# Two projections side by side on small weight pieces at the start, and five banks, paired stores and four tiles on GpSimd at the end of an encoder layer

## The chip, the cores and the metric

The kernel runs on one core of one Trainium2 chip. The metric is the device time of one execution in microseconds. Three executions of the kernel before took 2081.0, 2082.01 and 2082.91 us; the median is 2082.01 us. TensorE (PE), ScalarE (ACT), VectorE (DVE), GpSimd (POOL) and SyncE (SP, which here only issues DMAs) each work through an instruction queue of their own in order.

## The reference

One encoder layer on 512 tokens with 2048 features, all float32. Cut to what matters here:

```python
xn = rms_norm(x, attn_norm_g)
u_val, u_gate, q, k, v = split(xn @ w_in)          # 1024 + 1024 + 3 * 1024 columns
y_conv = silu(layer_norm(depthwise_conv31(u_val * sigmoid(u_gate))))
y_na = neighborhood_attention(q, k, v, rpb)        # 16 heads of 64, grid 8 x 64, window 8 x 16
x = x + concat(rms_norm(y_conv), rms_norm(y_na)) @ w_out
up = depthwise_conv3(rms_norm(x) @ w_up)           # 2 * 5632 columns
x = x + (silu(gate) * val) @ w_down                # gate, val = halves of up
return rms_norm(x, final_norm_g)
```

## The kernel before, in words

Everything is kept transposed: a tile is 128 features (partitions) by 512 tokens, so x is 16 tiles. Every matrix product is made in three matmuls of a reduced float32 format (`mm3`, L117): each operand is split into a high part (a copy on ACT, rounded to that format) and a low part (a subtraction on DVE), and high by high, high by low and low by high are accumulated in PSUM. A weight "unit" is 128 by 1024 numbers, 512 KB: `raw_unit` (L102) loads it through SP, `parts` (L106) makes its high part `whi` on ACT (L109) and its low part `wlo` on DVE (L110). Raw tiles have seven buffers, high and low parts four each. Units come from one list, `plan`, in the order of their use; `weights` (L141) makes three units ahead of the one that is used.

**Start** (L90, L202 to L251). The table of all parameters `prm` (344 KB) is loaded first. Then, in an order that is pinned, come the 16 tiles of x, each with its split `xh` (ACT, L210) and `xl` (DVE, L211), scaled by the norm's gain, which is read from `prm`. Behind tiles 0, 2, 6 and 15 one of the first four weight units is loaded and split whole: first half of the gate tile's weights, first half of the value tile's, then the second halves. `project` (L243) makes one tile of columns: two units, 8 by 3 matmuls each, 48 matmuls in all. After each unit `tick` (L127) issues one step of work that is waiting in `steps` and `asteps`. The first such step, `stats1` (L234), sums the squares of x: 16 squares on ACT and 15 additions on DVE, all handed over at the first tick, that is ahead of the fifth weight unit in the program. `rsqrt_steps` (L165) then turns the sums into 1/sqrt: two matmuls per 128 tokens, a chain of small DVE and ACT instructions, and a matmul that spreads the result over the partitions. `glu` (L258) projects a gate and a value tile; `gated` (L263) follows when the norm's factor is known, with 31 DVE instructions of a depthwise convolution at low priority.

**Middle**. `ORDER` (L50) says in which order the eight gated tiles ("a") and the eight head pairs ("q") are projected. `attend` (L346) is a generator: scores of two blocks, softmax on DVE and ACT, transposes (`turn`), products with the values, a step per tick. The output projection and the norm follow. The gated MLP runs in 11 chunks of four hidden tiles; `up` (L594) makes a hidden tile in seven products, and between the products `down` (L713) multiplies the chunk before by w_down: 12 matmuls for one of 16 feature tiles in one of two PSUM banks (tag "tr"), a copy `pdc` on ACT (L722), and a DMA of POOL that adds it to x in HBM (L723).

**End** (L733 to L771). After the seventh product of the last hidden tile, feature tiles 8 to 15 of the last but one chunk are still to be done by `down`, 96 matmuls in the two "tr" banks. Then the 16 tiles of x are read back from HBM (L741), the last chunk's weights are split into `dh` and `dl` (L750, L751), and each half of the tokens (256) goes through 16 feature tiles of 12 matmuls, an addition to x (DVE, L765), a square (ACT) and an addition of the square to `acc3` (DVE, L163). `rsqrt_of` gives the final norm's factor in PSUM, and `finish` (L753) multiplies a tile on DVE and stores it by SP, 128 KB a store: for the first half beside the matmuls of the second, for the second half at the very end.

Of the kernel before, what the change touches and what calls it, by code (L numbers as in the profile page):

```python
# [10 lines left out]
F32 = mybir.dt.float32  # L11
F32R = mybir.dt.float32r
# [33 lines left out]
AHEAD = 3  # L46
NW = 4
NEG = -1.0e30

ORDER = "aaaqqaqaaaqqaqqq"  # L50
# [14 lines left out]
def layer(ctx: ExitStack, tc: tile.TileContext, xT, w_in, w_out, w_up, w_down, par, tab, out):  # L65
# [23 lines left out]

    prm = consts.tile([P, NPAR], F32, name="prm")  # L90
    nc.sync.dma_start(prm, par)

    def pc(name, i):
        o = POFF[name] + i
        return prm[:, o:o + 1]
# [69 lines left out]
    def rsqrt_steps(acc, n, name, to=slice(0, S), keep=True):  # L165

        m = (to.stop - to.start) // P
        ps = psa.tile([P, 2, S], F32, tag="sc", name="st")[:, 0]
        for i in range(m):
            nc.tensor.matmul(ps[:, i:i + 1], acc[:, to.start + i * P:to.start + (i + 1) * P], ones[:, 0:1],  # L170
                             start=True, stop=True)
# [4 lines left out]
        nc.vector.tensor_mul(y, v, r)  # L176
        nc.vector.tensor_mul(y, y, r)
        nc.vector.tensor_scalar(y, y, -0.5, 1.5, op0=ALU.mult, op1=ALU.add)
        nc.vector.tensor_mul(y, y, r)

        dg = t2("dg")
        for i in range(m):
            nc.vector.tensor_scalar(dg[:, i * P:(i + 1) * P], ident, y[:, i:i + 1], None, op0=ALU.mult)
        yield
        ps = psa.tile([P, 2, S], F32, tag="sc", name="st")[:, 0]
        nc.tensor.matmul(ps[:, :m * P], ones, dg[:, :m * P], start=True, stop=True)
# [6 lines left out]
    def rsqrt_of(*a, **k):  # L193
        g = rsqrt_steps(*a, **k)
# [7 lines left out]
    xs, x1, early = [], [], []  # L202
    acc1 = t2("acc1")
    pin = tc.keep_in_program_order
    first = [w_in[n, :, u * U * P:(u + 1) * U * P] for u in range(KD // U) for n in (NC_, 0)]
    for k in range(KD):
        x1.append(t2("x"))
        last = pin(nc.sync.dma_start(x1[k], xT[k]))
        h, l = t2("xh", F32R), t2("xl", F32R)
        pin(nc.scalar.activation(h, x1[k], AF.Copy, scale=pc("g1", k)))  # L210
        pin(nc.vector.scalar_tensor_tensor(l, x1[k], pc("g1", k), h.bitcast(F32), op0=ALU.mult, op1=ALU.subtract))  # L211
        xs.append((h, l))
        if k in (0, 2, 6, 15):
            raw, i = raw_unit(first[len(early)], U * P)
            pin(i)
            w = parts(raw, U * P)
            pin(w[2])
            pin(w[3])
            early.append(w[:2])
    for i in (0, 2, 1, 3):  # L220
        plan.append(lambda i=i: early[i])
# [6 lines left out]
    del plan[4:8]  # L228
# [5 lines left out]
    def stats1():  # L234
        for k in range(KD):
            sum_sq(acc1, x1[k], k == 0)
        for _ in range(3):
            yield
        rstd.append((yield from rsqrt_steps(acc1, D, "rstd1")))
# [3 lines left out]
    def project(n):  # L243
        ps = psm.tile([P, S], F32, tag="mm", name="pj")
        for u in range(KD // U):
# [5 lines left out]
            while late:  # L251
                late.pop()()
        return ps

# [3 lines left out]
    def glu(i):  # L258
        pg, pv = project(NC_ + i), project(i)

        late.append(lambda: gated(i, pg, pv))
# [84 lines left out]
    def attend(p, q, k, v):  # L346
# [71 lines left out]
        scores(2)  # L418
        turn()
        yield  # L420
        values(0)
# [109 lines left out]
    nc.vector.tensor_scalar(fwn, prm[:, POFF["fww"] + 3 * NF:POFF["fww"] + 6 * NF], -1.0, None, op0=ALU.mult)  # L531
# [181 lines left out]
    def down(hs, ds):  # L713
# [12 lines left out]
    for c in range(NCH):  # L726
# [6 lines left out]
        if last:  # L733
            down(pend, down_units(c, i, 6))
        pend = hs
    hs = pend
    n = CH
    x2 = []
    for d in range(KD):
        xk = t2("x2")  # L740
        nc.sync.dma_start(xk, xd[d])  # L741
        x2.append(xk)

    ws = []
    for d0 in range(0, KD, 2):
# [7 lines left out]
    def finish(d, r, to):  # L753
        nc.vector.scalar_tensor_tensor(x2[d][:, to], x2[d][:, to], pc("g3", d), r, op0=ALU.mult, op1=ALU.mult)
        nc.sync.dma_start(out[d, :, to], x2[d][:, to])

    done = None
    for t0 in range(0, S, S // 2):
        to = slice(t0, t0 + S // 2)
        acc3 = t2("acc3")  # L760
        for d in range(KD):
# [4 lines left out]
            sum_sq(acc3[:, to], x2[d][:, to], d == 0, to=to)  # L766
            if done is not None:
                finish(d, *done)
        done = (rsqrt_of(acc3, D, "rstd3", to=to, keep=False), to)
    for d in range(KD):  # L770
        finish(d, *done)  # L771
# [62 lines left out]
```

## Time and profile before

| | |
|---|---|
| median of three executions | 2082.01 us |
| the profiled execution | 2080.55 us |
| its span, first to last instruction | 2078.8 us |
| PE busy | 2044.7 us |
| DVE, ACT, POOL busy | 1662.4, 1056.5, 153.4 us |
| granted TensorE clock, mean | 0.996 |

In the views, times are microseconds from the start of the span. A row of the timeline gives start, duration, engine, line, operation, output and inputs, shape, how many like it in a row were merged, and in brackets how long the engine was idle before it and what ended that. PEld is PE's loading of weights, which runs beside the matmuls. Matmul durations overlap: the distance from start to start is the pace. A row of the table of stretches gives for each engine the busy time and the count, then the granted clock, the share of the DMA engines' time and the GB/s moved.

### The profile page before, as it was taken

Reading aid. Unit: us, or ns where it says so; the run is one execution under the profiler, and the core shown is the slowest. Engines: PE = TensorE matmul, PEld = TensorE weight load, DVE = VectorE, ACT = ScalarE, POOL = GpSimd, SP = SyncE. Lnnn points to the kernel's source line nnn. Section 1 sums busy time; section 2 is a strip of 40 time slices with the busy share of each in tenths; the row PEclk is TensorE's granted clock in tenths of the full one; section 3 lists DMA queues with packets and bytes.
Section 4 is the critical chain, followed back from the end, with each engine's and each line's share of the span. In section 5 each row is a group of like instructions: output and inputs, shape, how many; then the busy total and the mean of one; then the engine's idle time right before and its main releaser. Section 6 shows DMA issues by size and latency. Waiting matters only on the chain.

```text
span 2078.8 us, 28526 instructions
## 1 busy us (share of the span) xinstructions
PE 2044.7 (98%) x10784; PEld 1729.8 (83%) x10784; DVE 1662.4 (80%) x2323; ACT 1056.5 (51%) x1712; POOL 153.4 (7%) x182
## 2 busy tenths in 40 slices
PE   8999999999999999999999999999999999999997
PEld 6888888887788898888888888888888888888876
DVE  7985797587577898888888888788887887879856
ACT  6234423447445545555555555554555555555542
POOL 0000000000001001111111111111111111110110
PEclk9999999999999999999999999999999999999998
DMA  6243223335337435566565565656556556554672
GB/s 229 81 133 101 92 82 112 102 101 184 133 112 176 128 113 137 127 147 146 114 151 142 132 135 141 136 127 153 134 129 147 138 130 144 142 127 120 149 193 82
DMA packets 98362, 275.37 MB, mean 132 GB/s; under 512 B 10929, under 2 KB 15025, under 8 KB 98225
## 3 DMA queue, kind: packets, MB, share of 16 engines
q1 hardware_dynamic: 73008, 227.40, 35.7%
q0 software_dynamic: 25216, 46.15, 15.3%
q8 instruction: 85, 1.39, 0.3%
q14 instruction: 53, 0.43, 0.1%
HBM read 218.98 MB, written 54.53 MB: 132 GB/s over the span
## 4 chain that ended last, share of the span: by engine, by line
issue 52%; PE 38%; POOL 6%; DVE 1%; DMA 1%; ACT 1%; POOLq 0%; SPq 0%; DVEq 0%; ACTq 0%
PE pj L120 7%; PE pj L122 7%; PE pj L121 7%; POOL x2d L723 6%; PE po L120 2%; PE po L121 2%; PE po L122 2%; PE pu L604 2%; PE pd L120 1%; PE pd L122 1%; PE pd L121 1%; PE pu L605 1%; PE sc L366 1%; PE po L409 1%; PE trp L396 1%
## 5 line engine op out<-in xcount | busy, mean ns | idle before, releaser
L604 PE MATMUL pu<-xc,whi 128*128 128x512 f32 x2240 | 782.5, 397 | 0.3 <-ACT pl L618 0.3
L110 DVE TENSOR_TENSOR wlo<-raw,whi 128x1024 fp32r<-128x1024 f32 x368 | 449.2, 1221 | 280.1 <-ACT whi L109 252.5
L109 ACT ACTIVATE whi<-raw 128x1024 fp32r<-128x1024 f32 x368 | 389.1, 1058 | 503.7 <-PE pj L121 216.5
L605 PE MATMUL pu<-xc,wlo 128*128 128x256 f32 x2240 | 583.0, 281 | 0.0
L604 PEld LDWEIGHTS pu<-xc,whi 128*128 128x128 f32 x2240 | 407.9, 188 | 80.4 <-ACT pl L618 0.6
L605 PEld LDWEIGHTS pu<-xc,wlo 128*128 128x128 f32 x2240 | 422.8, 189 | 25.5
L120 PE MATMUL pj<-xh,whi 128*128 128x512 f32 x640 | 253.5, 397 | 8.2 <-ACT whi L109 8.2
L120 PE MATMUL pd<-hh,whi 128*128 128x512 f32 x640 | 250.6, 392 | 4.0 <-ACT pdc L722 4.0
L122 PE MATMUL pj<-xh,wlo 128*128 128x512 f32 x640 | 250.0, 391 | 1.1 <-DVE wlo L110 1.0
L122 PE MATMUL pd<-hh,wlo 128*128 128x512 f32 x640 | 249.4, 392 | 1.4 <-DVE wlo L110 1.4
L121 PE MATMUL pj<-xl,whi 128*128 128x512 f32 x640 | 250.5, 392 | 0.0
L121 PE MATMUL pd<-hl,whi 128*128 128x512 f32 x640 | 249.6, 390 | 0.0
L723 POOL DMA_DIRECT2D x2d<-pdc x160 | 139.2, 872 | 1180.4 <-ACT pdc L722 1180.4
L618 ACT ACTIVATE pl<-pu 128x256 f32<-128x256 f32 x280 | 105.2, 381 | 178.8 <-PE pu L604 178.8
L109 ACT ACTIVATE whi<-ws 128x1024 fp32r<-128x1024 f32 x132 | 139.8, 1059 | 66.9 <-PE pu L604 41.7
L280 DVE SCALAR_TENSOR_TENSOR y<-ch,prm,y 128x507 f32<-128x507 f32 (+14 forms) x240 | 169.9, 739 | 3.1
L110 DVE TENSOR_TENSOR wlo<-ws,whi 128x1024 fp32r<-128x1024 f32 x132 | 161.0, 1219 | 1.1 <-ACT whi L109 1.0
L120 PEld LDWEIGHTS pj<-xh,whi 128*128 128x128 f32 x640 | 120.5, 188 | 36.4 <-ACT whi L109 9.5
L722 ACT ACTIVATE pdc<-pd 128x512 f32<-128x512 f32 x160 | 94.4, 591 | 106.9 <-PE pd L122 106.9
L122 PEld LDWEIGHTS pd<-hh,wlo 128*128 128x128 f32 x640 | 120.4, 188 | 30.1 <-DVE wlo L110 4.9
L122 PEld LDWEIGHTS pj<-xh,wlo 128*128 128x128 f32 x640 | 120.4, 188 | 28.3 <-DVE wlo L110 2.5
L120 PEld LDWEIGHTS pd<-hh,whi 128*128 128x128 f32 x640 | 120.7, 189 | 26.3 <-ACT pdc L722 4.4
(162 smaller groups left out, 2745.0 us busy)
## 6 DMA issues: line engine op xcount, KB each, us to landing
raw<-in_w_up SPq DMA_DIRECT2D x176, 512.0 KB, 3.7
raw<-in_w_down SPq DMA_DIRECT2D x88, 512.0 KB, 3.7
raw<-in_w_in SPq DMA_DIRECT2D x80, 512.0 KB, 3.8
x2d<-pdc POOLq DMA_DIRECT2D x160, 256.0 KB, 4.8
raw<-in_w_out SPq DMA_DIRECT2D x32, 512.0 KB, 3.7
x<-in_xT SPq DMA_DIRECT2D x32, 256.0 KB, 6.0
tab<-in_tab SPq DMA_DIRECT2D x32, 256.0 KB, 4.2
x2d<-x SPq DMA_DIRECT2D x16, 256.0 KB, 2.0
```

The lines of the kernel that those rows point to most:

```text
L109: i = nc.scalar.activation(hi[:, :n], raw[:, :n], AF.Copy)
L110: j = nc.vector.tensor_sub(lo[:, :n], raw[:, :n], hi[:, :n].bitcast(F32))
L120: nc.tensor.matmul(ps, hi[:, a], mh, start=start, stop=False)
L121: nc.tensor.matmul(ps, hi[:, a], ml, start=False, stop=False)
L122: return nc.tensor.matmul(ps, lo[:, a], mh, start=False, stop=stop)
L280: nc.vector.scalar_tensor_tensor(y[:, a:b], h[:, a + j - PAD:b + j - PAD], prm[:, o + j:o + j + 1], y[:, a:b], op0=ALU.mult, op1=ALU.add)
L366: m = nc.tensor.matmul(both[:, j, i, :], q[hp, b * P:(b + 1) * P], grid(k, KC0[b], KW)[hp], start=True, stop=True)
L604: wide = lambda: nc.tensor.matmul(ps, hi, m, start=k == 0, stop=k == U - 1)
L605: low = lambda: nc.tensor.matmul(ps[:, H:], lo, m[:, :H], start=False, stop=False)
L618: nc.scalar.activation(to, ps, AF.Copy)
L722: nc.scalar.activation(t, ps, AF.Copy)
L723: nc.gpsimd.dma_start(xd[d], t, accum_op=ALU.add)
```

## The change

The start: only the 16 gains `g1` of the first norm are loaded ahead, by a DMA of ACT; `prm` follows behind the last tile of x. ACT makes one small square and PE nine matmuls on a tile of ones as soon as that tile is set. The weights of the first two tiles come in pieces of 2, 2, 4, 4 and 4 of their 16 blocks, loaded and split behind tiles 0, 2, 4, 6 and 9 of x. `project_first` makes both tiles together: for each tile of x the three matmuls of the one and the three of the other, in the two "tr" banks, with a tick at every fourth. Three further weight units stand ahead of that in the program, and `stats1` hands over four squares and additions per tick.

The middle: `ORDER` changes, and for the first five head pairs `attend` does scores(2) after values(0).

The end: tiles 8 to 15 of `down` are spread over the two "tr" banks and the three banks of tag "mm"; the last chunk's weights are loaded and split between them, and x tiles 0 to 7 are read back ahead of them, 8 to 15 behind them. The last square is not added to `acc` on DVE but summed by further matmuls; two DVE instructions fewer stand in `rsqrt_steps`. `finish` handles two feature tiles with one store of 256 KB. At the very end tiles 2, 3, 8 and 9 are scaled by their gain on ACT and multiplied on GpSimd by a copy of the factor in SBUF.

```diff
-ORDER = "aaaqqaqaaaqqaqqq"
+ORDER = "aaqaqaqaaqaqaqqq"
...
+    g1 = consts.tile([P, KD], F32, name="g1")
+    pin(nc.scalar.dma_start(g1, par[:, POFF["g1"]:POFF["g1"] + KD]))
     prm = consts.tile([P, NPAR], F32, name="prm")
-    nc.sync.dma_start(prm, par)
...
-    def rsqrt_steps(acc, n, name, to=slice(0, S), keep=True):
+    def rsqrt_steps(accs, n, name, to=slice(0, S), keep=True):
...
-            nc.tensor.matmul(ps[:, i:i + 1], acc[:, to.start + i * P:to.start + (i + 1) * P], ones[:, 0:1],
-                             start=True, stop=True)
+            for acc in accs:
+                nc.tensor.matmul(ps[:, i:i + 1], acc[:, to.start + i * P:to.start + (i + 1) * P], ones[:, 0:1],
+                                 start=acc is accs[0], stop=acc is accs[-1])
...
-        nc.vector.tensor_mul(y, v, r)
-        nc.vector.tensor_mul(y, y, r)
-        nc.vector.tensor_scalar(y, y, -0.5, 1.5, op0=ALU.mult, op1=ALU.add)
-        nc.vector.tensor_mul(y, y, r)
+        nc.vector.scalar_tensor_tensor(y, r, -0.5, r, op0=ALU.mult, op1=ALU.mult)
+        nc.vector.tensor_mul(y, y, v)
+        nc.vector.scalar_tensor_tensor(y, y, 1.5, r, op0=ALU.add, op1=ALU.mult)
...
+    def piece(u, j, c0, c1):
...
+        pin(nc.sync.dma_start(raw, w_in[n, :, (u * U + c0) * P:(u * U + c1) * P]))
+        pin(nc.scalar.activation(hi, raw, AF.Copy))
+        pin(nc.vector.tensor_sub(lo, raw, hi.bitcast(F32)))
...
+    pin(nc.scalar.activation(idle, ones[:, 0:1], AF.Square))
+    ps = psa.tile([P, S], F32, tag="po", name="idle")
+    for _ in range(IDLE):
+        pin(nc.tensor.matmul(ps[:, :P], ones, ones, start=True, stop=True))
+    pieces = {k: [(u, j, c0, c1) for j in range(2)]
+              for k, u, c0, c1 in ((0, 0, 0, 2), (2, 0, 2, 4), (4, 0, 4, 8), (6, 1, 0, 4), (9, 1, 4, 8))}
...
+    with tc.issue_after(last.ins):
+        nc.sync.dma_start(prm, par)
...
+    def project_first():
+
+        while len(made) < AHEAD:
+            made.append(plan[len(made)]())
+        both = [psa.tile([P, S], F32, tag="tr", name="pj", bufs=2) for _ in range(2)]
+        for kk in range(KD):
+            for j in range(2):
+                m = mm3(both[j], early[j][kk // U][1:], kk % U, xs[kk][0], xs[kk][1], kk == 0, kk == KD - 1)
+            if kk % 4 == 3:
+                tick(m)
+        return both
...
-        scores(2)
-        turn()
-        yield
-        values(0)
+        if p < NORM_AT:
+            turn()
+            yield
+            values(0)
+            scores(2)
+            yield
+        else:
+            scores(2)
+            turn()
+            yield
+            values(0)
...
-    nc.vector.tensor_scalar(fwn, prm[:, POFF["fww"] + 3 * NF:POFF["fww"] + 6 * NF], -1.0, None, op0=ALU.mult)
+    with tc.issue_after(last.ins):
+        nc.vector.tensor_scalar(fwn, prm[:, POFF["fww"] + 3 * NF:POFF["fww"] + 6 * NF], -1.0, None, op0=ALU.mult)
...
-                ps = psa.tile([P, S], F32, tag="tr", name="pd", bufs=2)
+                ps = (psm.tile([P, S], F32, tag="mm", name="pd") if wide and d % 5 > 1 else
+                      psa.tile([P, S], F32, tag="tr", name="pd", bufs=2))
...
+    for d in range(KD // 2):
+        reload(d)
+    for d in down_units(NCH - 1, CH - 1, 6):
+        down(pend, (d,), wide=True)
+        last_weights(len(ws))
+        last_weights(len(ws))
+    for d in range(KD // 2, KD):
+        reload(d)
...
+        o = t2("fin").rearrange("p (i t) -> p i t", i=2)
+        for i in range(2):
+            x, g = x2[d + i][:, to], pc("g3", d + i)
+            if apart:
+                nc.scalar.activation(x, x, AF.Copy, scale=g)
+                nc.gpsimd.tensor_mul(o[:, i], x, r)
+            else:
+                nc.vector.scalar_tensor_tensor(o[:, i], x, g, r, op0=ALU.mult, op1=ALU.mult)
+        nc.sync.dma_start(out[d:d + 2, :, to].rearrange("d p t -> p d t"), o)
...
+            if d < KD - 1:
+                sum_sq(acc[:, to], x2[d][:, to], d == 0, to=to)
+            else:
+                q = t2("sq")
+                nc.scalar.activation(q[:, to], x2[d][:, to], AF.Square)
...
+    rb = t2("rb")[:, h1]
+    nc.scalar.activation(rb, r, AF.Copy)
+    for d in range(0, KD, 2):
+        apart = d in (2, 8)
+        finish(d, rb if apart else r, h1, apart)
```

More of the change, by code (lines that the diff above doesn't have):

```diff
@@ L163, in sum_sq @@
             nc.vector.tensor_add(acc, acc, q)
-    def rsqrt_steps(acc, n, name, to=slice(0, S), keep=True):
+    def rsqrt_steps(accs, n, name, to=slice(0, S), keep=True):
+        if not isinstance(accs, tuple):
+            accs = accs,
         m = (to.stop - to.start) // P
@@ L209, in layer @@
         h, l = t2("xh", F32R), t2("xl", F32R)
-        pin(nc.scalar.activation(h, x1[k], AF.Copy, scale=pc("g1", k)))
-        pin(nc.vector.scalar_tensor_tensor(l, x1[k], pc("g1", k), h.bitcast(F32), op0=ALU.mult, op1=ALU.subtract))
+        pin(nc.scalar.activation(h, x1[k], AF.Copy, scale=g1[:, k:k + 1]))
+        pin(nc.vector.scalar_tensor_tensor(l, x1[k], g1[:, k:k + 1], h.bitcast(F32), op0=ALU.mult, op1=ALU.subtract))
         xs.append((h, l))
[L213 to L221, printed above, removed]
+        for c in pieces.get(k, ()):
+            piece(*c)
+    with tc.issue_after(last.ins):
+        nc.sync.dma_start(prm, par)
     a_, q_ = iter(range(NC_)), iter(range(NP_))
@@ L236, in stats1 @@
             sum_sq(acc1, x1[k], k == 0)
-        for _ in range(3):
+            if k % 4 == 3:
+                yield
+        for _ in range(STAT_AT):
             yield
@@ L250, in project @@
             tick(m)
-            while late:
-                late.pop()()
-        return ps
+            while late and rstd:
+                late.pop(0)()
+        return ps
+    def project_first():
[8 more added lines that the diff above has]
+        return both
     ys, ypair = [], []
     def glu(i):
-        pg, pv = project(NC_ + i), project(i)
+        pg, pv = project_first() if i == 0 else (project(NC_ + i), project(i))
         late.append(lambda: gated(i, pg, pv))
@@ L732, in layer, with reload, last_weights @@
         hs = [in_two(h) for h in hs]
[L733 to L736, printed above, removed]
+        if not last:
+            pend = hs
     n = CH
[L738 to L745, printed above, removed]
+    x2, ws = [], []
+    def reload(d):
+        x2.append(t2("x2"))
+        nc.sync.dma_start(x2[d], xd[d])
+    def last_weights(d0):
         raw, _ = raw_unit(down_weights(NF - CH, d0), U * P)
@@ L752, in layer, with finish, half @@
             ws.append((h, l))
[L753 to L760, printed above, removed]
+    for d in range(KD // 2):
[6 more added lines that the diff above has]
+        reload(d)
+    def finish(d, r, to, apart=False):
+        o = t2("fin").rearrange("p (i t) -> p i t", i=2)
[7 more added lines that the diff above has]
+        nc.sync.dma_start(out[d:d + 2, :, to].rearrange("d p t -> p d t"), o)
+    def half(to, between):
+        acc = t2("acc3")
         for d in range(KD):
@@ L765, in layer, with first_half @@
             nc.vector.tensor_add(x2[d][:, to], x2[d][:, to], ps)
[L766 to L771, printed above, removed]
+            if d < KD - 1:
[3 more added lines that the diff above has]
+                nc.scalar.activation(q[:, to], x2[d][:, to], AF.Square)
+            between(d)
+        return rsqrt_steps((acc, q), D, "rstd3", to=to, keep=False)
+    h0, h1 = slice(0, H), slice(H, S)
+    stats, todo = half(h0, lambda d: None), list(range(0, KD, 2))
+    r0 = []
+    def first_half(d):
+        if d == 0:
+            next(stats)
+        elif d == 2:
+            try:
+                next(stats)
+            except StopIteration as e:
+                r0.append(e.value)
+        elif d > 2 and d % 5 != 4 and todo:
+            finish(todo.pop(0), r0[0], h0)
+    r = rsqrt_value(half(h1, first_half))
+    assert not todo
+    rb = t2("rb")[:, h1]
[3 more added lines that the diff above has]
+        finish(d, rb if apart else r, h1, apart)
 def _cols(a):
```

22 lines of the change are left out of this document (15 added, 7 removed).

## The prediction

> **What bounds the kernel now.** I read the page first, then the list of PE's waits, then the timeline of the first 50 us and of the last 100 us, engine by engine.
>
> ```profile
> PE 2044.7 (98%) x10784; PEld 1729.8 (83%) x10784; DVE 1662.4 (80%) x2323; ACT 1056.5 (51%) x1712; POOL 153.4 (7%) x182
> ```
>
> PE is busy for 2044.7 of the 2078.8 us of the span. So only some 34 us are open to a change that leaves the products alone, and the question is where they lie. The list of PE's waits (total, times, longest) says where PE stood with something to do:
>
> ```profile
> PE pj L120 <- ACT whi L109: 8.2, 1, 8.2
> PE pd L120 <- ACT pdc L722: 4.0, 1, 4.0
> PE st L186 <- DVE dg L183: 2.1, 1, 2.1
> PE st L170 <- DVE acc L163: 1.5, 1, 1.5
> PE pd L122 <- DVE wlo L110: 1.4, 8, 0.2
> PE trv L354 <- ACT pt L400: 1.4, 1, 1.4
> PE pd L120 <- ACT dh L750: 1.2, 1, 1.2
> PE pj L122 <- DVE wlo L110: 1.0, 1, 1.0
> ```
>
> Each large one occurs once: 8.2 us before the first matmul, 1.0 in the third tile, 1.4 in the attention, 4.0 and 1.2 near the end, 1.5 and 2.1 in the final norm; behind that lie the stores. The change touches nearly all these places. The 80% of DVE do not bind: PE waits for it only for single microseconds.
>
> **The start.** ACT's timeline, PE's, the table's DMA with its size and time to landing, and DVE's:
>
> ```profile
> 4.91 1.28 ACT L210 ACT_TABLE_LOAD   x1 [4.91 <-DMA x<-in_xT]
> 6.20 0.72 ACT L210 ACTIVATE xh<-x,prm 128x512 fp32r<-128x512 f32 x1
> 7.08 1.06 ACT L109 ACTIVATE whi<-raw 128x1024 fp32r<-128x1024 f32 x1 [0.15 <-DMA raw<-in_w_in]
> ```
> ```profile
> 8.19 0.79 PE L120 MATMUL pj<-xh,whi 128*128 128x512 f32 x1 [8.19 <-ACT whi L109]
> ...
> 12.00 0.39 PE L122 MATMUL pj<-xh,wlo 128*128 128x512 f32 x1
> ```
> ```profile
> prm<-in_par SPq DMA_DIRECT2D x1, 344.0 KB, 2.9
> ```
> ```profile
> 0.84 0.17 DVE L98 MEMSET ones<- 128x128 f32 x1 [0.84 <-PEq L826]
> 3.70 0.23 DVE L531 TENSOR_SCALAR fwn<-prm 128x132 f32<-128x132 f32 x1 [2.69 <-DMA prm<-in_par]
> 6.96 0.75 DVE L211 SCALAR_TENSOR_TENSOR xl<-x,prm,xh 128x512 fp32r<-128x512 f32 x1 [3.03 <-ACT xh L210]
> ```
>
> Before, the table (344 KB, SP's first DMA) takes 2.9 and releases `fwn` at 3.70, x tile 0 lands at 4.9, ACT then loads its function table for 1.28 us, and the first 512 KB weight unit is there only at 7.08. The change takes the table from the front, loads ACT's functions on the tile of ones (set at 1.0), and asks for 128 KB of weights instead of 512. In place of the table's 344 KB now stand tile 0 and the first piece, 384 KB: I take 3.4 for the one and 3.9 for the other, on the scale of 344 KB by 3.7. The 8 KB of gains on ACT's queue have no row; between 0 and the 2.9 us of the table they land by 3.7, with tile 0, and cost nothing. Then xh 0.72, to 4.1, and a high part of 256 columns, between a quarter of 1.06 and the whole; a quarter and overhead, 0.4. Data would let PE begin at 4.6.
>
> The nine matmuls on ones stand in front in PE's queue. The nearest rows are in the final norm:
>
> ```profile
> 2064.06 0.61 PE L170 MATMUL st<-ones,acc 128*128 128x1 f32 x4 [1.48 <-DVE acc L163]
> 2066.76 1.19 PE L186 MATMUL st<-dg,ones 128*128 128x256 f32 x2 [2.09 <-DVE dg L183]
> ```
>
> A full float32 matmul is two instructions. With one column two of them take 0.3 us, with 256 columns at the low clock 1.19. Nine of 128 columns from 1.1 on thus end between 3.8 and 11.8; half of 1.19 each, by columns, gives 6.5; since that 1.19 holds the run-out of a lone pair, I go below it, to 0.45 each, and 5.2. I take 5.3 for the first real matmul (4.6 to 6.5), 2.9 us ahead of 8.19.
>
> Clock: between the rows at 8.19 and 12.00 lie eight starts in 3.81 us, later ones come every 0.227 (88 from 12.00 to the row at 31.95 below); eight at that pace would be 1.81, so the slow beginning costs 2.0. After some 3.5 us of work the pace doubles. With PE at work from 1.1 the same 3.5 us end at about 4.6; I take 0.5 for what is left, between nothing and the 2.0 of now. The Trainium skill, TensorE: Matmul & The Clock Gate (Part 1, on the HAM clock gate), says that the clock rises after a busy window of about 3.4 us and that the windows run freely, not started by the kernel; the slow beginning here agrees. By it the full clock would come at an estimated 4.6 to 8.0, and from 5.3 on up to 1.4 would be lost, more or less from execution to execution; no row of one execution can show that spread.
>
> Do data hold PE up later? Before, the two tiles already run mixed: the doubled row
>
> ```profile
> 12.91 0.62 PE L120 MATMUL pj<-xh,whi 128*128 128x512 f32 x2
> ```
>
> is two tiles' products in turn, and at 0.227 from 12.00 on there is no pause. So "side by side" itself adds little. Per tile of x PE needs six matmuls, 1.36 us; ACT 0.72 + 2 x 1.06/8 = 1.0; DVE 0.75 and, by the columns of that row, 2 x 0.19 for the low parts, 1.1; and the DMA
>
> ```profile
> 15.00:20.00 5.00, 5.00 (x24) 4.14 (x23) 5.00 (x8) 5.00 (x9) 0.00 (x0) 1.00 1.06 396
> ```
>
> at 396 GB/s brings 256 + 128 KB in 1.0 us. PE stays the slowest. The first tiles come one after the other through ACT and DVE, for which I give back 0.4 (0 to 1). So the start brings 2.9 + 1.5 - 0.4 = **4.0 us** (1 to 5).
>
> The stall in the third tile:
>
> ```profile
> 31.95 0.39 PE L120 MATMUL pj<-xh,whi 128*128 128x512 f32 x1
> 32.17 0.39 PE L121 MATMUL pj<-xl,whi 128*128 128x512 f32 x1
> 33.60 0.50 PE L122 MATMUL pj<-xh,wlo 128*128 128x512 f32 x1 [1.04 <-DVE wlo L110]
> ```
> ```profile
> 23.75 8.66 DVE L163 TENSOR_TENSOR acc<-acc,sq 128x512 f32<-128x512 f32 x11
> ```
>
> 1.43 instead of 0.23 between two starts, because eleven additions stand before `wlo`. They were handed over ahead of that unit; now three units stand ahead of the sums in the program, and the first can be split once its data and a buffer are there, in the low twenties, while PE arrives at 28. **1.2 us** go (0 if the additions win). What is late next is the norm's factor: its matmuls are queued behind the second unit of that tile, some 11 us on, long enough for the additions that are left.
>
> **The middle.** The order and the scores leave the number of all instructions as it is. The only wait there that a row shows is the 1.4 of `trv`; it may go or come again at another place. The new order puts at most two convolutions behind each other where there were three, so DVE's backlog is no larger than one that PE passes now without a further wait. I take 0, from 1.4 gained to 3 lost (two such waits more).
>
> **The end.** PE's rows:
>
> ```profile
> 1991.14 0.39 PE L122 MATMUL pd<-hh,wlo 128*128 128x512 f32 x1
> 1995.48 0.79 PE L120 MATMUL pd<-hh,whi 128*128 128x512 f32 x1 [3.96 <-ACT pdc L722]
> ...
> 1998.50 0.39 PE L121 MATMUL pd<-hl,whi 128*128 128x512 f32 x1
> ```
> ```profile
> 1994.85 1.07 ACT L722 ACTIVATE pdc<-pd 128x512 f32<-128x512 f32 x2
> ```
> ```profile
> 2013.03 0.39 PE L122 MATMUL pd<-hh,wlo 128*128 128x512 f32 x1
> 2014.63 0.39 PE L120 MATMUL pd<-hh,dh 128*128 128x256 f32 x1 [1.21 <-ACT dh L750]
> ```
>
> Two banks are filled by 1991.14, and ACT is at the last hidden tile until 1994.85. Five banks hold 5 x 12 matmuls of 0.227, 13.6 us instead of 5.4, so PE has work until 1999.5, when ACT has copied the first ones out. The pause of 4.34 - 0.23 = 4.1 goes. After it the clock is low: seven starts from 1995.48 to 1998.50 take 3.02 instead of 1.59, another 1.4, which goes with the pause. The last chunk's weights are now split between the copies: 16 parts and 8 copies of some 0.5 us on ACT, 12 us from 1994.85, against 21.8 us of matmuls from 1986; so the 1.60 - 0.23 = 1.4 at 2013.03 go too. Behind these, x tiles 8 to 15 are read back once their additions in HBM have landed; eight feature tiles lie before the first of them is needed. Sum **6.9 us** (5.5, without the clock's part, to 6.9).
>
> **The final norm and the stores.** DVE's rows, and one stretch of the stores:
>
> ```profile
> 2063.58 0.42 DVE L163 TENSOR_TENSOR acc<-acc,sq 128x256 f32<-128x256 f32 x1 [0.54 <-ACT sq L162]
> ...
> 2065.34 0.16 DVE L176 TENSOR_TENSOR rsy<-rsv,rsr 128x2 f32<-128x2 f32 x1
> ...
> 2067.99 6.35 DVE L754 SCALAR_TENSOR_TENSOR x<-x,prm,st 128x256 f32<-128x256 f32 x16 [1.38 <-PE st L186]
> ```
> ```profile
> 2073.00:2074.00 1.00, 0.00 (x0) 0.00 (x0) 1.00 (x4) 0.00 (x0) 0.00 (x0) 0.50 0.79 265
> ```
>
> The last addition goes, 2063.58 to 2064.06, 0.48, against some two more of the four small matmuls of 0.61 behind the square: 0.2 net. One DVE instruction less in the chain (five become four): 0.2. Then DVE has 12 products of 0.40 instead of 16, and GpSimd four. The multiplication on GpSimd has no row; I take 0.6 (0.4 as on DVE to 1.3), after a copy of 0.4, so its pairs are done 1.7 and 2.9 us after the factor, DVE's last after 4.8. The Trainium skill, GPSIMD Engine Reference (Performance versus the Vector engine), calls that engine the wrong choice for elementwise work, about half as fast; by its cycles a tile would take an estimated 0.6 to 0.7. Even 1.3 would not set the end.
>
> What does is the stores: 2.1 MB at 265 GB/s with 79% of the DMA engines' time. After, the first store waits for two products, 0.4 later, and SP's queue may stand 0.3 behind GpSimd's pair. If stores of 256 KB fill the engines, 265/0.79 = 335 GB/s, the flow takes 6.3 instead of 7.9: 0.9 won. At 396, the loads' rate, 2.2; at an unchanged 265, 0.7 lost. I take 0.9. Sum **1.3 us** (-0.3 to 2.6).
>
> **Sum.** 4.0 + 1.2 + 0 + 6.9 + 1.3 = 13.4. The profiled execution took 2080.55, 1.75 more than its span, and becomes 2067.15. The median before is 1.46 higher than that execution, and nothing in the change takes that away: 2082.01 - 13.4 = **2068.6**.
>
> **Rivals.**
> *The early start does not come* (0.15): the ones hold PE until 6.5 or more, or the clock's slow beginning is paid in full again, or the small pieces land late because 26 issues of some 0.4 us, 10 us in all, replace 20. The start then brings 1 instead of 4: 2071.6. For it speaks that each of the three is a bound and not a row; against it that the work from 1.1 on is as dense as what raised the clock before.
> *The stores stay at their rate* (0.12): 265 GB/s is the flow, not the issue; the tail brings -0.3: 2070.2. For it speaks that the DMA engines are 79% busy already.
> *A new wait in the middle* (0.09): moving the head pairs forward brings attention beside the first convolutions; 4 us more, three waits like the 1.4 of `trv`: 2072.6.
> *Slower: the late table blocks DVE* (0.06). `fwn` reads the table and stood at 3.70, before the first `xl`. If it keeps that place in DVE's queue, every `xl` and `wlo` is queued behind it, and PE behind those, until the table lands after all of x and the pieces: 6.6 MB at 396 GB/s from 2 us on is 18.8. PE then begins its pairs at some 20 instead of 8.2, at the low clock again, with ACT's and DVE's splits for the next units and the sums all pressed behind: the first two tiles end at 20 + 21.8 + 1.5 = 43 instead of 31.95, and a stall of 2 to 4 us follows in the third. 11 + 3 lost against 8.2 won at the end: 2087. It decides once `fwn` stands before the third `xl`. Against it: the change ties it to the last tile of x.
>
> **How the numbers follow.** The forecast has the rest, 0.58. The range takes the bounds of the terms: all of them good give 2082.0 - 5 - 1.2 - 1.4 - 6.9 - 2.6 = 2065, and the clock's chance under the median 2 more, 2063; the start at 1 and the stall kept, 2 lost in the middle, 5.5 and 0 at the end, give 2077, but not together: 2075. 0.2%, 4.2 us, is about what a measurement of this kernel can tell from no change. Faster by more: all but the last rival and a part of the middle's, 0.91; within 0.2%: 0.05; slower: 0.04.
>
> **What would show it.** Right: the first matmul on `whi` near 5.3 and the third tile's near 28; no PE wait on `pdc` and a clock of 1.00 from there on; PE's last product some 12 us earlier; eight stores at over 300 GB/s. Wrong: `fwn` before `xl` on DVE, PE waits on DVE in the first 20 us, new rows of PE waits between 40 and 600, or a wait for `dh` or for x read back in the last 60 us.

## The result, and the profile after

| | before | after |
|---|---|---|
| median | 2081.51 us (4 executions) | 2067.55 us (4 executions) |
| the profiled execution | 2080.55 us | 2068.61 us |
| its span | 2078.8 us | 2066.8 us |

The ratio is 0.9935, with a 95% interval from 0.9923 to 0.9947: 13.96 us less by the medians, 12.0 by the two spans. The profiled execution of after is the longest of its four. Cut at the same matmuls, by their starts in PE's timeline, the 12.0 us lie here:

| stretch | before, us | after, us | difference | predicted |
|---|---|---|---|---|
| to the third tile's first product | 31.95 | 29.18 | -2.77 | -4.0 |
| from there to the last `pj` | 467.86 | 467.61 | -0.25 | -1.2 and 0 |
| last `pj` to the first `pu` | 193.06 | 193.09 | +0.03 | 0 |
| first to last `pu` | 1292.80 | 1291.46 | -1.34 | 0 |
| last `pu` to the last `pd` | 76.63 | 69.44 | -7.19 | -6.9 |
| from there to the end | 16.47 | 16.06 | -0.41 | -1.3 |

So the sum came as forecast, the terms only in part. The list of PE's waits, after (what waited, for what; total, times, longest):

```profile
PE st L193 <- DVE dg L190: 1.9, 1, 1.9
PE trv L390 <- ACT pt L436: 1.4, 1, 1.4
PE pd L127 <- DVE wlo L115: 1.4, 8, 0.2
PE idle L229 <- DVE ones L103: 1.1, 1, 1.1
PE pj L125 <- DVE gate L301: 1.0, 2, 0.6
```

The 8.2 us at the start, the 4.0 for `pdc`, the 1.2 for `dh` and the 1.0 for `wlo` have left the list. New are the wait for the tile of ones, which only precedes the nine matmuls, and the last row, a wait of `pj` for DVE's `gate`. PE's timeline of the start, after:

```profile
1.05 4.21 PE L229 MATMUL idle<-ones 128*128 128x128 f32 x18 [1.05 <-DVE ones L103]
4.92 0.66 PE L125 MATMUL pj<-xh,whi 128*128 128x512 f32 x1
...
15.72 0.39 PE L127 MATMUL pj<-xh,wlo 128*128 128x512 f32 x1
16.48 0.73 PE L125 MATMUL pj<-xh,whi 128*128 128x512 f32 x2 [0.37 <-ACT xh L237]
...
29.18 0.39 PE L125 MATMUL pj<-xh,whi 128*128 128x512 f32 x1
```

The first real product comes at 4.92. From there 96 products of 0.227 us would end at 26.7; they end at 29.18, so 2.5 us went into slow starts and pauses. One pause is from 15.72 to 16.48: PE waits there for ACT's split of the next tile of x, which stands behind a weight piece that ACT had waited for until it landed. The end, after: DVE, ACT and GpSimd, then the list of SP's waits:

```profile
2056.48 4.79 DVE L817 SCALAR_TENSOR_TENSOR fin<-x,prm,st 128x256 f32<-128x256 f32 x12 [1.79 <-ACT rb L856]
```
```profile
2056.07 0.38 ACT L856 ACTIVATE rb<-st 128x256 f32<-128x256 f32 x1 [2.68 <-PE st L193]
```
```profile
2056.53 2.78 POOL L815 TENSOR_TENSOR fin<-x,rb 128x256 f32<-128x256 f32 x4 [49.58 <-ACT rb L856]
```
```profile
SPq L818 <- POOL fin L815: 7.7, 1, 7.7
```

Two things to see. DVE's first product stands behind ACT's copy of the factor, although it doesn't read the copy; both read the factor in the same PSUM tile. And the first store in SP's queue is that of GpSimd's pair, which is ready at 57.94 (two tiles of 0.70 from 56.53), while DVE's first pair is ready at 57.35. Before, the first store was issued 0.51 us after DVE's first product, now 1.49 (57.97).

### The profile page after: what moved, and what is told of

Read it like the earlier page. It is cut to its first block, busy times and chain, and to the rows that moved or that the text cites. A ratio compares the mean times of both kernels' runs of the same rounds, so it can differ in the third digit from the quotient of the medians.

```text
span 2066.8 us, 28555 instructions
## 1 busy us (share of the span) xinstructions
PE 2046.6 (99%) x10810; PEld 1733.0 (84%) x10810; DVE 1664.6 (81%) x2316; ACT 1065.4 (52%) x1728; POOL 156.2 (8%) x186
## 4 chain that ended last, share of the span: by engine, by line
issue 52%; PE 39%; POOL 6%; DMA 1%; DVE 1%; ACT 1%; SPq 0%; POOLq 0%; DVEq 0%; ACTq 0%
PE pj L125 7%; PE pj L126 7%; PE pj L127 7%; POOL x2d L769 6%; PE po L125 2%; PE po L126 2%; PE po L127 2%; PE pu L648 2%; PE pd L125 1%; PE pd L127 1%; PE pd L126 1%; PE pu L649 1%; PE sc L402 1%; PE trp L432 1%; PE po L445 1%
## 5 line engine op out<-in xcount | busy, mean ns | idle before, releaser
L115 DVE TENSOR_TENSOR wlo<-raw,whi 128x1024 fp32r<-128x1024 f32 x364 | 444.2, 1221 | 252.4 <-ACT whi L114 231.1
L114 ACT ACTIVATE whi<-raw 128x1024 fp32r<-128x1024 f32 x364 | 384.3, 1058 | 471.7 <-PE pj L126 177.1
L316 DVE SCALAR_TENSOR_TENSOR y<-ch,prm,y 128x508 f32<-128x508 f32 (+14 forms) x240 | 172.9, 740 | 4.1
L126 PEld LDWEIGHTS pd<-hl,whi 128*128 128x128 f32 x640 | 120.2, 188 | 25.7
L126 PEld LDWEIGHTS pj<-xl,whi 128*128 128x128 f32 x640 | 120.3, 188 | 25.6 <-DVE xl L238 1.2
```

Of the source, the lines that this page charges most:

```text
L114: i = nc.scalar.activation(hi[:, :n], raw[:, :n], AF.Copy)
L115: j = nc.vector.tensor_sub(lo[:, :n], raw[:, :n], hi[:, :n].bitcast(F32))
L126: nc.tensor.matmul(ps, hi[:, a], ml, start=False, stop=False)
L316: nc.vector.scalar_tensor_tensor(y[:, a:b], h[:, a + j - PAD:b + j - PAD], prm[:, o + j:o + j + 1], y[:, a:b], op0=ALU.mult, op1=ALU.add)
```

## The experiments

The time of each kernel is the median of its own executions; for some edits a microsecond decides, and there the intervals (about 1.5 us to either side, or more) don't separate the kernels. Then the rows decide, and the text says so. One mark is used often: the start of the third tile's first product.

**The end: the banks.**

```diff
-        down(pend, (d,), wide=True)
+        down(pend, (d,))
```

> As after, but tiles 8 to 15 of down at the end stay in the two tr banks. Theory (the banks are what removed the pause): a PE wait on pdc of about 4 us comes back behind the last hidden tile, with seven slow starts (about 1.4 us) behind it; last pu to last pd 69.4 + 5.5 = 75 us, the kernel 4.3 to 5.7 us slower than after, about 2072 to 2073. Rival (the splitting of the last weights between the copies and the early read-back made the gain): no wait over 1 us, under 1.5 us slower.

2073.96 us, ratio 0.9969 (0.9959 to 0.9979). PE's timeline has the pause again:

```profile
1986.36 0.39 PE L127 MATMUL pd<-hh,wlo 128*128 128x512 f32 x1
1990.70 0.50 PE L125 MATMUL pd<-hh,whi 128*128 128x512 f32 x1 [3.95 <-ACT pdc L768]
```

Between the two starts lie 4.34 us, to the hundredth what lay there before the change. Last `pu` to last `pd` takes 75.25 instead of 69.44: 5.8 us more. So the five banks alone make 5.8 of the 7.2, pause and slow clock, and the earlier splitting and read-back about 1.4, which was the size given to the gap at `dh`. The kernel is 6.4 us slower than after by the medians, more than the 4.3 to 5.7 expected. The rival falls.

**The end alone** (the kernel before with all edits from `rsqrt_steps` and `down` on, and with none of the others).

> The kernel before with only the end of the change (five banks, early splitting and read-back, paired stores, GpSimd, the shorter norm). Theory (start and end are independent): 6.9 to 7.2 at the banks and 0.4 to 0.8 in the tail, 7.3 to 8 us faster than before. Rival (part of the end's gain depends on the start or the order): under 6 us faster.

2072.5 us, ratio 0.9966 (0.9954 to 0.9978), 8.7 us faster by the medians. The interval, 4.6 to 9.6 us, would leave room for the rival; the trace does not: last `pu` to last `pd` is 69.4 here too, 7.2 less than before, and the tail 0.5 less. The end needs neither the start nor the order. Theory held.

**The tail without GpSimd.**

```diff
-    rb = t2("rb")[:, h1]
-    nc.scalar.activation(rb, r, AF.Copy)
     for d in range(0, KD, 2):
-        apart = d in (2, 8)
-        finish(d, rb if apart else r, h1, apart)
+        apart = False
+        finish(d, r, h1)
```

> As after, but all 16 last products are on DVE and the factor is not copied to SBUF. Theory (the copy of the factor holds DVE's first product back by 0.4, and the flow of the stores, not DVE, sets the end): DVE starts its products within 0.1 us of the last matmul on dg, the store flow starts about 0.4 earlier, the end comes 0 to 0.4 us earlier (kernel 0 to 0.4 faster than after). Rival (DVE's 16 products at 0.4, 6.4 us, would be the bound, so GpSimd is needed): the end comes 0.8 to 1.6 us later.

2066.75 us (2066.0 to 2067.19), ratio 0.9933 (0.9916 to 0.9949). DVE's timeline, then a stretch of the flow (engines' busy time, clock, DMA share, GB/s):

```profile
2055.19 6.36 DVE L817 SCALAR_TENSOR_TENSOR fin<-x,prm,st 128x256 f32<-128x256 f32 x16 [1.31 <-PE st L193]
```
```profile
2059.00:2060.00 1.00, 0.00 (x0) 0.00 (x0) 1.00 (x4) 0.00 (x0) 0.00 (x0) 0.50 1.02 333
```

DVE now waits 1.31 for PE instead of 1.79 for ACT, and the first store is issued 0.90 us after the first product instead of 1.49. The sixteen products end at 2061.55, and the stores go on past that, at 333 GB/s with the DMA engines' time full (share 1.02). From the last `pd` product to the end it takes 15.13 us instead of 16.06, and the matmul that spreads the factor, just ahead of the first product, ran slowly in both (1.13 and 1.19 us), so the two tails can be compared. So GpSimd's four tiles did not bring the gain of the tail; they cost it some 0.9 us, by their copy and their place at the head of SP's queue, more than the 0 to 0.4 expected. The time alone would not prove it.

**Single stores.**

```diff
-        nc.sync.dma_start(out[d:d + 2, :, to].rearrange("d p t -> p d t"), o)
+            nc.sync.dma_start(out[d + i, :, to], o[:, i])
```

> As after, but each feature tile of 128 KB is stored by itself. Theory (the larger stores raised the flow from 265 to 340 GB/s): the flow at the end falls to about 268 GB/s, the first store starts 0.4 earlier, the kernel is 0.8 to 1.6 us slower than after. Rival (the flow follows from other things, such as the work that stood beside it): rate above 320 GB/s, time within 0.4 us of after.

2068.67 us, ratio 0.9948 (0.9933 to 0.9963). A stretch of its flow:

```profile
2059.00:2060.00 1.00, 0.00 (x0) 0.00 (x0) 1.00 (x3) 0.00 (x0) 0.00 (x0) 0.50 0.82 268
```

268 GB/s at a share of 0.82, as before the change; the packets are as large as in after, only the stores are half as large. From the first issue to the end of the span it takes 10.36 us, with pairs 8.87, before the change 10.27. So the size of the store sets the flow, and that is worth 1.4 to 1.5 us. Not all of it reaches the end, since a single store leaves sooner: 0.80 us behind the first product instead of 1.49. The matmul that spreads the factor took 0.67 us here; beside the kernel with the old order and twenty ones below, where it took 0.67 too and the stores are pairs, the tail is 0.8 longer (16.35 against 15.54). Theory held.

**The order.**

```diff
-ORDER = "aaqaqaqaaqaqaqqq"
+ORDER = "aaaqqaqaaaqqaqqq"
...
-        if p < NORM_AT:
+        if False:
```

> As after, but with the old ORDER and the old order of scores and values in the attention. Theory (the two new waits of pj on DVE's gate, 1.0 and 0.6 us, come from the new order, which is worth nothing otherwise): those waits vanish, the kernel is 0 to 1.5 us faster than after. Rival (the new order brings a gain that the profile does not show as a wait): 1 us or more slower than after.

2078.42 us, ratio 0.9988 (0.9979 to 0.9998): 10.9 us slower than after. The two waits for `gate` do vanish, but the theory, that the order was worth nothing otherwise, is wrong by far. PE's timeline, then DVE's:

```profile
96.45 0.39 PE L126 MATMUL pj<-xl,whi 128*128 128x512 f32 x1
105.91 0.79 PE L127 MATMUL pj<-xh,wlo 128*128 128x512 f32 x1 [9.07 <-DVE wlo L115]
106.50 0.63 PE L125 MATMUL pj<-xh,whi 128*128 128x512 f32 x1
```
```profile
76.73 9.30 DVE L316 SCALAR_TENSOR_TENSOR y<-ch,prm,y 128x510 f32<-128x510 f32 x14
85.95 0.68 DVE L368 TENSOR_TENSOR q<-pj,rstd 128x512 f32<-128x512 f32 x1
86.56 9.91 DVE L316 SCALAR_TENSOR_TENSOR y<-ch,prm,y 128x506 f32<-128x506 f32 x15
...
104.64 2.35 DVE L115 TENSOR_TENSOR wlo<-raw,whi 128x1024 fp32r<-128x1024 f32 x2
```

Between 76.7 and 104.6 DVE works almost only on convolutions, and the low part that PE needs at 96.45 stands behind them. Before the change the same backlog was there, with the same pair of low parts behind it:

```profile
80.88 9.28 DVE L280 SCALAR_TENSOR_TENSOR y<-ch,prm,y 128x506 f32<-128x506 f32 x14
...
99.61 2.36 DVE L110 TENSOR_TENSOR wlo<-raw,whi 128x1024 fp32r<-128x1024 f32 x2
```

They came 5.0 us earlier there, and PE came 4.2 later: 3.0 at the third tile and 1.2 by the stall. 5.0 + 4.2 = 9.2, what lies between the starts at 96.45 and 105.91 over the pace. Seven slow starts behind it cost another 1.5. The 5.0 come for the most part from the first norm's factor, which DVE's first `gate` waits for until 48.04 instead of 43.59: the sums now make way for the weights, and the last of them starts at 42.00 instead of 36.94. So before the change the three convolutions just fitted, with nothing to spare: PE's matmul there starts at 100.89, 0.28 behind the one ahead of it.

> The kernel before with nothing but the new ORDER and the new place of scores(2). Theory (the order only protects: with the late start DVE's backlog of convolutions just fits, and only an earlier PE runs into it): within 1.5 us of before, no wait of PE on wlo near 90 to 110 us. Rival (the order saves PE time in any case): 4 us or more faster than before.

The two edits of the order on the kernel before: 2081.21 us against 2081.24, ratio 1.0002 (0.9992 to 1.0011), and no wait for `wlo`. The order is worth nothing with the late start and 10.9 us with the early one. And without it the early start does harm: the old order with the new start and end stands 5.9 us behind the end alone (2078.42 against 2072.5).

```diff
-        if p < NORM_AT:
+        if False:
```

> As after, with the new ORDER, but scores(2) back ahead of values(0) for all head pairs. Theory (ORDER alone keeps the 9.1 us wait on wlo away, and the two waits of pj on gate come from the scores behind values, whose table is asked for behind a weight unit that waits for its buffer, with the gate behind them on DVE): no PE wait on gate and none on wlo; 0.3 to 1.5 us faster than after. Rival (the place of the scores protects too): a PE wait of 2 us or more between 50 and 400 us, slower than after.

2068.12 us, ratio 0.9946 (0.993 to 0.9963). No wait for `wlo`: ORDER alone keeps it away. The waits for `gate` are gone, too, but another has come, of `po` for `pt`, 0.98 us at 117.90, and the time doesn't tell the kernel from after. The mechanism of the `gate` waits held, the gain did not come. The mechanism at the first of the two waits in after, in SP's timeline and in DVE's:

```profile
173.89 6.66 SPq L109 DMA_DIRECT2D raw<-in_w_in  x2
180.61 0.42 SPq L408 DMA_DIRECT2D tab<-in_tab  x1
```
```profile
185.06 0.69 DVE L412 SCALAR_TENSOR_TENSOR s<-sc,tab 128x512 f32<-128x512 f32 x1 [2.11 <-DMA tab<-in_tab]
185.67 0.68 DVE L301 TENSOR_TENSOR gate<-pj,rstd 128x512 f32<-128x512 f32 x1
```

The table of scores(2) is asked for at 180.61, behind a weight unit on SP that takes until then; DVE stands 2.11 us for it; `gate`, which frees a PSUM bank, is queued behind.

Against the kernel with the old order and nine ones:

```diff
-IDLE = 9
+IDLE = 20
```

> The kernel with the old order of tiles and scores, with 20 instead of 9 matmuls on ones, so that PE begins about 4 to 5 us later. Theory (with the old order DVE's chain of three convolutions sets the time there, and PE's early start only turns into waiting): the wait for wlo near 97 us shrinks by what PE starts later, and the kernel stays within 1 us of the old order with nine (2078.4). Rival (the wait is PE's own loss, whatever its start): the wait stays near 9 us and the kernel comes 3 us or more later.

The old order with eleven more matmuls on ones: 2079.28 us, ratio 0.9995 (0.9985 to 1.0005). This run did not answer its question. PE's first real product came 2.0 us later, at 6.92, not 4 to 5, because the later ones run at the full clock (0.11 us from start to start of their halves behind 3.98, 0.21 ahead of it); and the third tile came at 28.82, where the old order with nine had it at 28.91. PE was as early as with nine, and the wait for `wlo` is again 9.1. Which of the two halves weighs what is thus worked out from rows, not tried. But the run showed something else: starting 2.0 us later cost nothing at the third tile, since PE then never paused and started at the full pace. Up to a first product near 6.9, if PE is at full pace then, it is not that product that sets the mark: what is won ahead of it goes into slow starts and waits for data.

**The start: the ones.**

```diff
-IDLE = 9
+IDLE = 0
```

> As after, but without the nine matmuls on ones. Theory (they bring the clock): first real matmul at about 4.9, unchanged or a few tenths earlier, but the first seven to eight starts at twice the pace time, so that the third tile begins 1 to 2.5 us later and the kernel is 1 to 2 us slower. Rival (the first tiles wait for their data in any case, which hides the slow clock): third tile within 0.4 us of after, no difference.

2067.72 us, ratio 0.994 (0.9926 to 0.9955). PE's timeline:

```profile
4.91 0.79 PE L125 MATMUL pj<-xh,whi 128*128 128x512 f32 x1 [4.91 <-ACT whi L221]
...
10.28 0.89 PE L125 MATMUL pj<-xh,whi 128*128 128x512 f32 x2
11.00 0.40 PE L126 MATMUL pj<-xl,whi 128*128 128x512 f32 x1
```

Thirteen starts at 0.43 to 0.6 us, the last at 10.28, then the full pace. The third tile comes at 29.64; the six kernels that keep the new start unchanged have it at 28.37 to 29.18, mean 28.78. So the ones bring 0.9 us at that mark, between the rival's 0.4 and the theory's 1 to 2.5, since PE would wait for data in part of that time anyway. In the kernel's time it doesn't show: the last `pj` starts at 496.22, in the kernel without GpSimd, which has the ones, at 496.12. The waits for `gate` are as good as absent here. That is not for PE's later start: the kernel with the table first has the third tile later still, at 30.27, and 1.4 us of them. The table that `gate` stands behind landed 3.9 us after it was asked for here, 4.4 in after. So these waits differ from execution to execution, and an early gain of 0.9 can be hidden by them.

**Larger first pieces.**

```diff
-((0, 0, 0, 2), (2, 0, 2, 4), (4, 0, 4, 8), (6, 1, 0, 4), (9, 1, 4, 8))
+((0, 0, 0, 4), (3, 0, 4, 8), (6, 1, 0, 4), (9, 1, 4, 8))
```

> As after, but the first halves of the first two tiles' weights come in two pieces of four blocks (256 KB, rows of 2 KB) behind x tiles 0 and 3, instead of pieces of 2, 2 and 4 blocks. Theory (small pieces bring the first product early, but PE then waits for what follows; the data set the third tile): first real product 0.4 to 0.8 later than 4.92, fewer pauses between 5 and 8.5, the third tile at 28.4 to 29.2 as after, no difference in time. Rival (the small pieces are what makes the start early): third tile 0.8 us or more later and the kernel as much slower. Second rival (1 KB rows slow the DMA engines in that stretch): over 250 GB/s from 4 to 5 us, third tile earlier than 28.3.

2066.99 us, ratio 0.9933 (0.9918 to 0.9948). The same microsecond of after and of this kernel:

```profile
4.00:5.00 1.00, 1.00 (x7) 1.00 (x6) 0.44 (x1) 0.84 (x2) 0.00 (x0) 1.00 0.34 86
```
```profile
4.00:5.00 1.00, 1.00 (x6) 0.97 (x5) 0.52 (x1) 0.91 (x2) 0.00 (x0) 1.00 0.70 176
```

The flow dips there in all eight kernels with the first pieces of after, to between 35 and 156 GB/s; the second kernel with 256 KB, the last one below, has 154, so the two sizes are not told apart by that microsecond. By 9 us 2.25 and 2.12 MB had moved with 256 KB, 1.72 to 2.03 in the eight. The first real product comes at 5.23, 0.3 later, the third tile at 28.41, within the spread of after. No difference in time: the theory held, the small pieces win nothing and lose nothing that can be measured. Neither sign of the second rival came.

**The table first.**

```diff
     prm = consts.tile([P, NPAR], F32, name="prm")
+    pin(nc.sync.dma_start(prm, par))
...
-    with tc.issue_after(last.ins):
-        nc.sync.dma_start(prm, par)
```

> As after, but the 344 KB parameter table is SP's first DMA again. Theory (the table ahead costs its own transfer): first real product 0.9 to 1.3 later than 4.92, third tile about 1 us later, kernel 0.5 to 1.2 slower than after. Rival (the start is bound by ACT, DVE or the ones, not by what is loaded first): first real product and third tile within 0.3 us of after.

2068.22 us, ratio 0.9941 (0.9926 to 0.9956). First real product at 6.61, 1.7 later; third tile at 30.27, 1.5 later than the mean of 28.78. The table ahead costs about that, somewhat more than expected; in time 0.7 by the medians, which alone would prove nothing. Part of it is the clock: the ones are over by 5.3, PE stands 1.34 us, and eight starts of 0.43 to 0.59 us follow. With twenty ones up to 6.9, and PE at full pace at once, the same mark came at 28.82.

**All together**: no GpSimd, larger pieces, the first two tiles stored singly, and the tables of scores(2) asked for ahead of the transposes.

```diff
+        def tables(b0):
+            for j in range(2):
+                tb = t2("tab").rearrange("p (i k) -> p i k", i=2)
+                i = nc.sync.dma_start(tb, tab[2 * p + j][:, b0 // 2:b0 // 2 + 2])
...
         if p < NORM_AT:
+            tables(2)
             turn()
...
+            if apart:
+                nc.sync.dma_start(out[d + i, :, to], o[:, i])
+        if not apart:
+            nc.sync.dma_start(out[d:d + 2, :, to].rearrange("d p t -> p d t"), o)
```

> As after, with what the runs suggest: all last products on DVE, the first two feature tiles of the last half stored by themselves, the larger first pieces, and the tables of scores(2) asked for ahead of the transposes instead of behind them. Theory (the waits for the copy of the factor, for a table behind a weight unit, and the first store's wait for two tiles each cost what the rows show): no PE wait on gate (0.6 to 1.6 us), DVE's first last product 0.1 us behind the spread, flow of the stores at about 335 GB/s from 1.4 us behind it; 1 to 2.5 us faster than after, about 2065.5. Rival (these small waits only hide others of the same size): within 0.8 us of the kernel without GpSimd, 2066 to 2067.5.

2066.44 us (2065.67 to 2067.9, five executions), ratio 0.9934 (0.9921 to 0.9948). From PE's list of waits, and DVE's timeline:

```profile
PE sc L414 <- DVE s L421: 1.3, 1, 1.3
```
```profile
2053.93 6.36 DVE L823 SCALAR_TENSOR_TENSOR fin<-x,prm,st 128x256 f32<-128x256 f32 x16 [0.85 <-PE st L193]
```

No wait for `gate` is left, and the 1.4 of `trv` is gone, but one of 1.3 of `sc` has come. From the third tile to the first `pu` it takes 659.4 us, 1.3 less than in after and 0.9 less than without GpSimd. The first store goes out 0.51 us behind the first product, and the last `pd` product to the end takes 14.70 us, the shortest of all. But that is the clock, as the matmul that spreads the factor shows, without GpSimd and here, in PE's timeline:

```profile
2054.02 1.13 PE L193 MATMUL st<-dg,ones 128*128 128x256 f32 x2 [1.89 <-DVE dg L190]
```
```profile
2053.22 0.67 PE L193 MATMUL st<-dg,ones 128*128 128x256 f32 x2 [1.88 <-DVE dg L190]
```

From DVE's first product to the end of the span it is 9.9 us in both: the first store leaves 0.4 sooner, and the flow, nine stores instead of eight, takes 0.4 longer. So in the tail the single stores won nothing, as the rival has it, and in the middle one execution is 0.9 shorter, as the theory has it. By the medians the kernel is 0.3 us below the one without GpSimd and 1.1 below after; the intervals separate none of them.

## Why the prediction was right, and where its terms were not

2068.6 was forecast, 13.4 us less; 2067.55 came, 13.96 less. Its mechanisms for the start, the stall and the banks held. The terms:

*The end, 6.9:* right. 7.2 in the two traces; 5.8 with the banks alone undone, where pause and clock were put at 5.5. The slow clock's part is not the same in every execution: the order alone, whose end is that of before, took 77.8 us from last `pu` to last `pd` where before took 76.63.

*The start, 4.0:* right as a sum, in part by luck. In the two profiled executions the third tile moved by 2.8 only. But those are an early one of before and the latest of after. Three kernels with the old start (before, the order alone, the end alone) have that mark at 31.95, 34.23 and 32.67, mean 32.95; the six with the new one at 28.78; the difference is 4.2. But the term was worked out from the rows of the one execution at 31.95, and beside that one the six come to 3.2; the rest of the 4.2 is that the old start scatters, and the execution worked from was an early one. The step that was mis-sized is what the clock and the data still cost, 0.5 and "I give back 0.4 (0 to 1)": together they are 1.7 to 2.5, from 26.7 for a run at full pace to 28.37 to 29.18. On the other side the first product came at 4.92 instead of 5.3. The ones took 0.43 each where 0.45 was forecast, but without them it came at 4.91: the weights' high part was ready only then, so the data, put at 4.6, set it as much as the ones.

The old start with the order alone shows why the old start scatters:

```profile
9.51 0.80 PE L122 MATMUL pj<-xh,whi 128*128 128x512 f32 x1 [9.51 <-ACT whi L111]
...
14.77 0.56 PE L124 MATMUL pj<-xh,wlo 128*128 128x512 f32 x1
```

1.3 us later than before's 8.19 by its data, and twelve slow starts instead of seven. The slow time behind the first product is 3.6 us in the one execution, 5.7 in the other. The Trainium skill, TensorE: Matmul & The Clock Gate (Part 1, on the HAM clock gate), says that the clock's windows of about 3.4 us run freely, so that the same kernel can have 6, 11 or 14 slow matmuls; by that rule the slow time would lie between an estimated 3.4 and 6.8 us. The runs agree. The forecast took the median of before as its base, 1.46 above the profiled execution, on the ground that "nothing in the change takes that away". The marks speak against that: with the old start they lie 2.3 us apart, with the new one 0.8.

*The stall, 1.2, and the middle, 0:* together 0.25 came in the two traces. The stall of 1.04 is gone; two waits for `gate`, 1.36 us over the pace, came in its place. The rival "a new wait in the middle" was right in kind and a third of its size. What is behind those waits was not in the forecast at all: scores(2), moved behind values(0), ask for their table behind a weight unit on SP. The step "The order and the scores leave the number of all instructions as it is" was not followed to the DMA that moves with them. Little else changed in the middle. Take the time from the third tile to the first `pu` without PE's waits for `gate` (and without the 0.98 for `pt`, with the old scores): it is 659.6 to 659.9 us in eight kernels with the new order and the new start. The other side of the stall's cure, the factor that comes 4.5 us later because the sums make way, was counted as "long enough for the additions that are left"; for DVE's convolutions it is half of the 9.2 us under the old order.

*The order* was costed at nothing, since DVE's backlog would be "no larger than one that PE passes now without a further wait". That was true, and it hid what the edit does: the backlog with the old order fits only with the late start. By itself the order is worth 0.0, under the early start 10.9. A reader of the forecast could have dropped the edit as useless and lost most of what the change gives.

*The tail, 1.3:* 0.4 came. The chain gave its 0.2 and 0.2 (one DVE instruction fewer stands in it, not two), and the flow rose to some 340 GB/s, near the 335 forecast, and took 1.4 less from the first issue on. What failed is the two costs set at 0 and at 0.4 to 0.7: "after a copy of 0.4" was counted for GpSimd only, but held DVE back, +0.41; and the first store came 0.98 later behind the first product, 0.4 for the pair and 0.6 for GpSimd's pair ahead of it. -0.2 - 0.2 + 0.41 + 0.98 - 1.40 is the -0.41 of the table. GpSimd's multiplication, put at 0.6, took 0.70. The Trainium skill, GPSIMD Engine Reference (Performance versus the Vector engine), keeps to VectorE for elementwise work; by its 2.6 cycles an element a tile would take an estimated 0.6 to 0.7 on GpSimd. The trace agrees, 0.70 against DVE's 0.40. The rival of unchanged stores falls.

*First to last `pu`, -1.34:* not forecast. Three small waits of PE around 700 us are smaller after. The order alone has 1292.1 there, the kernels with the new start 1290.8 to 1291.6, the end alone 1296.05, in an execution 5.1 us above its median. No run was made for it; the cause stays open.

*The late table:* `fwn` stood behind the last tile of x, at 23.87 us on DVE. The slower rival falls. (Its own sum gives 2088, 2082 + 11 + 3 - 8.2, not 2087.)

## What to carry to other kernels

An edit that is worth nothing alone can be the one that lets another's gain through: ask of each engine off the critical path how much sooner it could be reached, and undo such an edit inside the changed kernel, not only add it to the old one. A transfer that is asked for later can stand behind other transfers in its queue, and whatever is queued on the engine that waits for it stands there too. To give part of a last burst of work to another engine costs its copies and its place in the queue of stores; here, where the stores were the bound, that is all it did. And the tails of two executions can be compared only where the last matmuls ran at the same clock: half a microsecond of clock looked like a gain of an edit here.

## What the runs showed of the hardware

- Stores of 128 KB flow at 264 to 273 GB/s with 0.8 of the DMA engines' time, stores of 256 KB at 331 to 347 with all of it, though each row of both is 1 KB (256 columns of float32).
- DVE did not begin to read a PSUM tile until ACT's copy from the same tile had ended: 1.79 us of waiting with the copy, 1.31 without. Whether the chip or the program's own order makes it so was not tried.
- Between 4 and 5 us of the span the flow of the loads is low: 35 to 156 GB/s in the eight kernels with loads of 128 KB among the first ones, 154 and 176 in the two with 256 KB. With the old start (units of 512 KB) it is 184, 188 and 303. Size, length of the rows and order changed together, so the cause stays open.
- At the end the clock falls at different times behind PE's last full work. The spread of the factor in PE's timeline, with the larger pieces and in after:

```profile
2053.26 0.82 PE L193 MATMUL st<-dg,ones 128*128 128x256 f32 x2 [1.89 <-DVE dg L190]
```
```profile
2054.83 1.19 PE L193 MATMUL st<-dg,ones 128*128 128x256 f32 x2 [1.88 <-DVE dg L190]
```

The granted clock was 0.83 in the microsecond of the first and 0.50 in that of the second. DVE's first product thus came 5.34 and 5.71 us behind the last `pd` product. Over the nine kernels with this same tail, last `pd` to the end takes 15.3 to 16.1 us.
